# Transformer blocks with a product-key expert layer on one core: order of the first loads, place of the picks' transpositions, output of the first gathered group

## The chip, the cores and the metric

One Trainium2 chip, one core, one program. The time is that of one execution on the device, in microseconds (us). TensorE (PE) multiplies, VectorE (DVE) and ScalarE (ACT) work elementwise, GpSimd (POOL) issues indirect loads, SyncE (SP) issues plain ones; 16 DMA engines move the bytes.

## What is computed

256 tokens of width 1024, a memory of 256 rows, all in float32. A first block adds three branches (a convolution, differential attention, cross attention to the memory), a second one mixes stick-breaking attention and a linear recurrence, and then comes the expert layer, which takes more than half of the time:

```python
h = rms_norm(x, norm_g); mem_h = rms_norm(mem, mem_norm_g)
k, v = jnp.split(mem_h @ w_mem_kv, 2, axis=-1)            # v is the first thing the kernel computes
...
top_s, top_i = lax.top_k(s, PEER_TOPK)                    # per token and head: 16 of 128 keys, twice
best_s, best_pos = lax.top_k(cand_s, PEER_TOPK)           # 16 of 256 pairs
idx = jnp.take_along_axis(cand_i, best_pos, axis=-1)      # 8 heads x 16 picks of 16384 experts
g = jax.nn.softmax(best_s, axis=-1)
u = jnp.take(expert_u, idx, axis=0); v = jnp.take(expert_v, idx, axis=0)
act = jax.nn.gelu(jnp.einsum('td,thkd->thk', xc, u))
y = jnp.einsum('thk,thkd->td', g * act, v)
```

## The kernel before

All work is laid out by a scheduler that fixes one order of instructions for each engine from the program text; each engine then runs its list in order and waits where an operand or a buffer isn't ready.

**Weights of the two blocks.** 94 blocks of weights, two tiles `raw` of 128x1024 (512 KB) each, are loaded by SP (L242). ScalarE rounds a tile to its high part `whi` (L248), VectorE forms the rest `wlo` (L249); four buffers of each are there, so a cast waits until TensorE is through with the tile two blocks back. A product of 256 columns is 48 matmuls of 128x256: high by high, high by low, low by high, over eight channels c (`linN` L343 to L345 for activations as the stationary side, `linT` L309 to L311).

**Start.** SP loads the memory `m_t` (four quarters of 256 KB), the vector `VT` of gains, the two tiles of weight block 0, the input `xr` in two halves, the constants `CT` and `ident`, then further weights. ScalarE scales m_t by its gains to `mgh` (L414), VectorE forms `mgl` (L415). The sums of squares of m_t are eight matmuls against ones (L441) into `stat`; `rstd_of` (L376 to L382) makes `rm` of them, and `tok_scalar` (L422, L424) turns it by token to `rmt`. Four calls of `linN` give the four pieces of `vm`, scaled by `rmt` when ScalarE copies them out (L505). In the second piece lie the sums of squares of xr (L399), then the normed input h, column by column: `nrm` (L409, VectorE), `hh` (L386, ScalarE) and `hl` (L386, VectorE), which the next products need.

**Expert layer.** 160 tokens are done densely: 64 blocks of `u` (`linP`, L290, `ga` takes the gelu) and 64 of `v` (`v_pair`, L1187, into `y`); the weight tiles `w` come in a ring of 13. The gates are applied through one-hot products (`A`, `B`, L1145 to L1165), 40 groups of eight tokens. The 96 other tokens are gathered: GpSimd fetches for each of 96 steps 128 rows of u and of v (L1196, 512 KB a step) into eight slots (three `gat`, five `gat2`), VectorE forms dots (L1203) and then sums (L1219, L1221), in order, over two groups of 32 and 64. Two lists put such work in between the blocks: `bg`, in which each piece has a cost and is popped at 4.6 a block of u, and `advance`, which moves the gathers on.

**Picks.** For each half of the tokens (t = 1, then 0) `bg` holds `logits`, two `decode` (4.3 each, they form the index tiles `IDX`, L1040) and `gates` (3.0), which makes the softmax and then turns both index tiles and the gates by three transpositions on TensorE (L1063 to L1065) and five copies on VectorE (L1067 to L1072).

**End.** `rows_out` is called before the third block of v from the end. For both groups it adds the residual to the sums: eight transpositions of xG (L1247) and a product with `fold` (L1249) into two `lin` tiles of PSUM, copies to a `gat` tile (L1251) and an output DMA from GpSimd (L1252). The dense part is copied from y by ScalarE (L1302) and VectorE (L1304) and written by SP (L1305).

Of the kernel before, what the change touches and what calls it, by code (L numbers as in the profile page):

```python
# [9 lines left out]
F32 = mybir.dt.float32  # L10
# [9 lines left out]
P = 128  # L20
# [168 lines left out]
def build(tc, xT, memT, vec, con, con0, wcat, rgw, keysT, u, v, urow, vrow, out):  # L189
    nc = tc.nc  # L190
    es = ExitStack()
    with es:
# [42 lines left out]
        def prep(i):  # L235
# [4 lines left out]
            for a in range(2):  # L240
                raw = spool.tile([P, 1024], F32, name="raw", bufs=5)
                nc.sync.dma_start(raw, srcs[i][:, a * 1024:(a + 1) * 1024])  # L242
# [89 lines left out]
        def linN(act):  # L332

            ah, al = act
            hs, ls = block()
            ps = lin_ps[0].tile([P, 2, T], F32, name="lin")
            for t in range(2):
                for c in range(8):
                    wh = hs[c // 4].rearrange("p (c j) -> p c j", c=4)[:, c % 4]
                    wl = ls[c // 4].rearrange("p (c j) -> p c j", c=4)[:, c % 4]  # L340
                    xh = ah[:, c, t * P:(t + 1) * P]
                    xl = al[:, c, t * P:(t + 1) * P]
                    nc.tensor.matmul(ps[:, t], xh, wh, start=c == 0, stop=False)  # L343
                    nc.tensor.matmul(ps[:, t], xh, wl, start=False, stop=False)  # L344
                    nc.tensor.matmul(ps[:, t], xl, wh, start=False, stop=c == 7)  # L345
            ahead()
            return ps
# [118 lines left out]
        with ExitStack() as e1:  # L466
# [15 lines left out]
            nc.sync.dma_start(m_t[:, 0:2], memT[:, 0:2])  # L482
            nc.sync.dma_start(VT, vec)
            for k in range(1, 4):
                nc.sync.dma_start(m_t[:, 2 * k:2 * k + 2], memT[:, 2 * k:2 * k + 2])
            prep(0)
            for k in range(2):
                nc.sync.dma_start(x_t[:, 4 * k:4 * k + 4], xT[:, 4 * k:4 * k + 4])
            nc.sync.dma_start(CT, con)
            nc.sync.dma_start(ident, con0[:, :P])  # L490
            mgh, mgl = bigt("mgh", F32R), bigt("mgl", F32R)
            for c in range(NC):
                gain_col(m_t, "mem_norm_g", mgh, mgl, c)
            rm = smt("rm", T, 1)
            stm = statp()
            for c in range(0, NC, 2):
                rms_sq(m_t, stm, c, NC)
# [13 lines left out]
            nc.vector.tensor_scalar_mul(GT[:, 0:1], V("diff_qn_g"), 0.125)  # L511
# [816 lines left out]
```

## Time and profile before

| | us |
|---|---|
| median of three runs | 1287.76 |
| lowest, highest | 1286.37, 1290.27 |
| the profiled execution | 1290.27 |
| its span in the trace | 1288.5 |
| busy: TensorE, VectorE, ScalarE, GpSimd | 1252.9, 936.7, 457.4, 219.3 |

The profile is of one execution. Busy time counts instructions from start to end; matmuls overlap, so a full TensorE shows as a share near 1 and its pace is read from the starts of neighbours or from counts in a window. In a row of the timeline the bracket at the end gives the idle time ahead of it and what ended that.

### The profile page before, as it was taken

The page shows a single profiled execution, that of the slowest core. Times are in us where ns is not written, and L with a number is a line of the kernel's source. Part 1 is how long each engine was busy: PE and PEld are TensorE (multiplying, and loading weights), DVE is VectorE, ACT ScalarE, POOL GpSimd, SP SyncE. Part 2 cuts the span into 40 slices and gives each one's busy share as a digit, 9 for nine tenths or more (in the row PEclk, how much of TensorE's full clock was granted, in tenths as well). Part 3 has the DMA queues.
Part 4 walks back from the last instruction along what each step waited for, and adds up shares of the span by engine and source line. Part 5 has one row for each costly group of instructions (what it writes and reads, how often), then busy time and mean ns, then how long its engine had stood idle before and what let it go on. Part 6 is the DMA issues. An engine that isn't in the chain of part 4 may idle for free.

```text
span 1288.5 us, 24481 instructions
## 1 busy us (share of the span) xinstructions
PE 1252.9 (97%) x9948; PEld 1211.2 (94%) x9948; DVE 936.7 (73%) x1806; ACT 457.4 (35%) x741; POOL 219.3 (17%) x232
## 2 busy tenths in 40 slices
PE   8999999999999999998999999999999999999995
PEld 7999999989999999977999999999999999999884
DVE  6789988888998776865899874678545876454542
ACT  7545677578646556964432111000100000000001
POOL 0000000000000000002013453222342225333330
PEclk9999999999999999999999999999999999999998
DMA  8555544434565664415677899999999999999994
GB/s 287 191 186 188 168 134 131 122 125 148 164 194 167 188 206 156 154 59 200 236 245 220 298 373 408 408 408 404 378 392 334 352 348 407 409 409 409 409 408 155
DMA packets 94865, 340.76 MB, mean 264 GB/s; under 512 B 10576, under 2 KB 12048, under 8 KB 94624
## 3 DMA queue, kind: packets, MB, share of 16 engines
q1 hardware_dynamic: 65312, 232.73, 51.0%
q0 software_dynamic: 29440, 106.46, 21.6%
q8 instruction: 78, 1.28, 0.4%
q14 instruction: 35, 0.29, 0.1%
HBM read 338.01 MB, written 1.05 MB: 263 GB/s over the span
## 4 chain that ended last, share of the span: by engine, by line
PE 43%; issue 19%; DMA 18%; DVE 10%; POOL 6%; ACT 3%; POOLq 0%; SPq 0%; DVEq 0%; ACTq 0%
DMA gat<-in_vrow,gi 13%; PE lin L310 10%; PE lin L309 10%; PE lin L311 10%; POOL gat L1196 5%; DMA gat<-in_urow,gi 5%; PE lin L343 1%; PE lin L345 1%; PE lin L344 1%; DVE gat L1203 1%; DVE acc L1221 1%; DVE wlo L249 1%; PE stat L461 1%; DVE s L997 1%; ACT whi L248 1%
## 5 line engine op out<-in xcount | busy, mean ns | idle before, releaser
L1187 PE MATMUL y<-ga,w 128*128 128x160 f32 x2048 | 292.9, 302 | 5.2 <-DMA w<-in_v 2.5
L1187 PEld LDWEIGHTS y<-ga,w 128*128 128x128 f32 x2048 | 279.9, 190 | 12.5 <-DMA w<-in_v 11.5
L249 DVE TENSOR_TENSOR wlo<-raw,whi 128x1024 fp32r<-128x1024 f32 x188 | 229.3, 1222 | 64.0 <-ACT whi L248 63.3
L290 PE MATMUL lin<-h3f,w 128*128 128x160 f32 x1888 | 265.4, 300 | 0.0
L290 PEld LDWEIGHTS lin<-h3f,w 128*128 128x128 f32 x1888 | 257.7, 190 | 0.2 <-issue 0.2
L248 ACT CAST whi<-raw 128x1024 fp32r<-128x1024 f32 x188 | 196.2, 1049 | 167.0 <-PE lin L310 125.7
L310 PE MATMUL lin<-hl,whi 128*128 128x256 f32 x704 | 200.2, 284 | 0.0
L311 PE MATMUL lin<-hh,wlo 128*128 128x256 f32 x704 | 199.8, 284 | 0.0
L309 PE MATMUL lin<-hh,whi 128*128 128x256 f32 x704 | 199.7, 284 | 0.0
L1221 DVE SCALAR_TENSOR_TENSOR acc<-gat,cG,acc 128x1024 f32<-128x1024 f32 x94 | 120.7, 1284 | 95.9 <-DMA gat<-in_vrow,gi 95.5
L1203 DVE CUSTOM_DVE_ANT_0 gat<-gat,hrow 128x1024 f32<-128x1024 f32 x96 | 116.1, 1223 | 28.6 <-DMA gat<-in_urow,gi 28.6
L311 PEld LDWEIGHTS lin<-hh,wlo 128*128 128x128 f32 x704 | 132.6, 188 | 2.2 <-issue 1.9
L310 PEld LDWEIGHTS lin<-hl,whi 128*128 128x128 f32 x704 | 132.6, 188 | 1.8 <-issue 1.4
L309 PEld LDWEIGHTS lin<-hh,whi 128*128 128x128 f32 x704 | 132.5, 188 | 1.4 <-issue 1.0
L1196 POOL DMA_INDIRECT gat<-in_urow,gi x96 | 101.5, 1058 | 181.2 <-DVE sG L1203 169.4
L1196 POOL DMA_INDIRECT gat<-in_vrow,gi x96 | 93.8, 977 | 166.1 <-DVE acc L1221 137.8
L1176 ACT ACTIVATE ga<-lin 128x320 f32<-128x320 f32 x64 | 28.0, 438 | 243.8 <-PE lin L290 239.5
L950 POOL DMA_DIRECT2D ga<-in_u x10 | 5.4, 545 | 601.3 <-DMA raw<-in_wcat 597.7
L537 DVE SCALAR_TENSOR_TENSOR cacc<-ub,VT,cacc 128x256 f32<-128x256 f32 x240 | 104.0, 480 | 0.0
L1302 ACT COPY ga<-y 128x160 f32<-128x160 f32 x4 | 1.2, 293 | 251.1 <-PE y L1187 251.1
L1165 DVE SCALAR_TENSOR_TENSOR ga<-gp,ga 128x256 f32<-128x256 f32 (+1 forms) x60 | 29.1, 511 | 63.3 <-PE gp L1154 55.9
L310 PE MATMUL lin<-h3lo,whi 128*128 128x256 f32 x128 | 37.6, 294 | 3.0 <-DVE h3lo L386 3.0
(376 smaller groups left out, 2152.0 us busy)
## 6 DMA issues: line engine op xcount, KB each, us to landing
raw<-in_wcat SPq DMA_DIRECT2D x188, 512.0 KB, 4.1
w<-in_v SPq DMA_DIRECT2D x128, 512.0 KB, 13.6
w<-in_u SPq DMA_DIRECT2D x118, 512.0 KB, 9.8
ga<-in_u POOLq DMA_DIRECT2D x10, 512.0 KB, 10.8
gat<-in_urow,gi POOLq DMA_INDIRECT x96, 8.9
gat<-in_vrow,gi POOLq DMA_INDIRECT x96, 18.8
m_t<-in_memT SPq DMA_DIRECT2D x4, 256.0 KB, 3.9
xr<-in_xT SPq DMA_DIRECT2D x2, 512.0 KB, 9.1
```

Source lines behind the costliest of these rows:

```text
L248: nc.scalar.copy(h, raw)
L249: state["sub"] = nc.vector.tensor_sub(l, raw, h.bitcast(F32))
L290: nc.tensor.matmul(ps[:, a], ws[a][:, c * P:(c + 1) * P], x[:, c], start=c == 0, stop=c == 7)
L309: nc.tensor.matmul(ps[:, a], wh, ah[:, c], start=(a, c) in first, stop=False)
L310: nc.tensor.matmul(ps[:, a], wh, al[:, c], start=False, stop=False)
L311: nc.tensor.matmul(ps[:, a], wl, ah[:, c], start=False, stop=(a, c) in last)
L537: nc.vector.scalar_tensor_tensor(cacc[:, c], s, w, cacc[:, c], op0=ALU.mult, op1=ALU.add)
L1165: state["dve"] = nc.vector.scalar_tensor_tensor(g_[:, :, tl], p_, 1.0 / GSCALE, g_[:, :, tl], op0=ALU.mult, op1=ALU.mult)
L1187: nc.tensor.matmul(yT[c // 2][:, c % 2, :D], ws[a][:, c * P:(c + 1) * P], g[:, a], start=False, stop=i == 63 and (a, c % 2) == (1, 1))
L1196: nc.gpsimd.indirect_dma_start(g, None, src, bass.IndirectOffsetOnAxis(gi[:, 0, k:k + 1].bitcast(U32), 0))
L1203: nc.vector.tensor_tensor_reduce(out=g, in0=g, in1=h, scale=1.0, scalar=0.0, op0=ALU.mult, op1=ALU.add, accum_out=sG[:, k:k + 1])
L1221: state["sum"] = nc.vector.scalar_tensor_tensor(acc[m], g, cG[:, k:k + 1], acc[m], op0=ALU.mult, op1=ALU.add)
```

## The change

First, the start. SP loads VT, one quarter of m_t, the first weight tile, two quarters, the second weight tile, the last quarter, both tiles of block 1, and only then xr, CT and ident. The first call of `linN` runs channel by channel (c outside, t inside). The sums of squares of the three later quarters are added on VectorE first, so eight matmuls against ones become four, the last two of them behind the first piece of vm; `rstd_of` and `tok_scalar` follow there. Small preparations (GT, lp) are held back behind a `wlo`, and the table of the second block's recurrence (`la`, `lb`) behind the gate of the merge. Second, `gates` is cut in two: `gates` at a cost of 1.2, a pause of 4.6 for t = 0 in the list, and `turn`, with the transpositions, at 1.8. Third, `rows_out` is cut into `rows_in` (transpositions) and `rows_out` (fold, copies, two output DMAs a group, issued by ScalarE); group 0 goes out in the midst of v, eight steps after its sums are complete, group 1 has `rows_in` at block 61 and `rows_out` behind the dense outputs.

```diff
-        def linN(act):
+        def linN(act, channelwise=False):
...
+            if channelwise:
+                seq = [(t, c) for c in range(8) for t in range(2)]
...
-            nc.sync.dma_start(m_t[:, 0:2], memT[:, 0:2])
             nc.sync.dma_start(VT, vec)
-            for k in range(1, 4):
-                nc.sync.dma_start(m_t[:, 2 * k:2 * k + 2], memT[:, 2 * k:2 * k + 2])
-            prep(0)
+            m_load(0)
+            raws = [load(0, 0)]
+            m_load(1)
+            m_load(2)
+            raws.append(load(0, 1))
+            m_load(3)
+            raws1 = [load(1, a) for a in range(2)]
             for k in range(2):
                 nc.sync.dma_start(x_t[:, 4 * k:4 * k + 4], xT[:, 4 * k:4 * k + 4])
...
+            for k in range(1, 4):
+                q = msq[min(k, 2)]
+                nc.scalar.square(q.rearrange("p (a b) -> p a b", a=2), m_t[:, 2 * k:2 * k + 2])
+                if k > 1:
+                    nc.vector.tensor_add(msq[1], msq[1], q)
...
-            rstd_of(stm[:, :T], 1.0 / 1024, T, out=rm)
-            rmt = tok_scalar(rm, "rmt")
...
-                ps = linN((mgh, mgl))
+                ps = linN((mgh, mgl), j == 0)
+                if j == 0:
+                    for b in range(2):
+                        nc.tensor.matmul(stm[:, :T], ONES, msq[1][:, b * T:(b + 1) * T], start=False, stop=b == 1)
+                    rstd_of(stm[:, :T], 1.0 / 1024, T, out=rm)
+                    rmt = tok_scalar(rm, "rmt")
...
-                bg.append((3.0, gates(t)))
+                bg.append((1.2, gates(t)))
                 if t:
                     bg.append((0.3, rows_index))
+                else:
+                    bg.append((4.6, lambda: None))
+                bg.append((1.8, turn(t)))
...
+            def rows_out(m):
+
+                o_, g, _ = groups[m]
+                o = rows.tile([P, 1024], F32, name="gat", tag="gat", bufs=NB)
+                for n, ps in enumerate(box["out", m]):
+                    sl = slice(n * 512, (n + 1) * 512)
+                    nc.tensor.matmul(ps[:g], fold[:, o_:o_ + g], acc[m][:, sl], start=False, stop=True)
+                    box["copied"] = nc.scalar.copy(o[:g, sl], ps[:g])
+                    nc.scalar.dma_start(out[D * 1024:].rearrange("(r d) -> r d", d=1024)[o_:o_ + g, sl], o[:g, sl])
...
-            if i + 64 == LAST + 1:
-                rows_out()
+            if box["first"] and box["n"] >= NG + GROUPS[0] + NB + MORE + 8:
+                box["first"] = False
+                rows_in(0)
+                rows_out(0)
+            if i == 61:
+                rows_in(1)
             v_pair(i)
...
+        rows_out(1)
```

The order on ScalarE from the statistics of xr (`rv`) to the last column of hh, before (`whi` are casts of weights, `vm` the copies of the pieces):

```order
L376 ACTIVATE rv<-stat,VT 128x256
L377 ACTIVATE rs<-rv 128x256
L378 ACTIVATE rs<-rs 128x256
L379 ACTIVATE rt<-rs 128x256
L248 CAST whi<-raw 128x1024
L505 ACTIVATE vm<-lin,rmt 128x256 x2
L248 CAST whi<-raw 128x1024
L386 CAST hh<-nrm 128x256 x2
L248 CAST whi<-raw 128x1024
L386 CAST hh<-nrm 128x256 x2
L505 ACTIVATE vm<-lin,rmt 128x256 x2
L248 CAST whi<-raw 128x1024
```

Four more hh, two casts of weights and the last two vm follow there. The same place now:

```order
L542 ACTIVATE vm<-lin,rmt 128x256 x2
L387 ACTIVATE rv<-stat,VT 128x256
L388 ACTIVATE rs<-rv 128x256
L389 ACTIVATE rs<-rs 128x256
L390 ACTIVATE rt<-rs 128x256
L254 CAST whi<-raw 128x1024
L397 CAST hh<-nrm 128x256
L254 CAST whi<-raw 128x1024
L397 CAST hh<-nrm 128x256
L542 ACTIVATE vm<-lin,rmt 128x256 x2
L559 ACTIVATE le<-stat 128x2
L397 CAST hh<-nrm 128x256 x6
```

The statistics stand behind the copies of the third piece instead of the first, and six of eight hh behind those of the fourth.

On TensorE, the transpositions of t = 0 among the matmuls of the u blocks, before (`ga_7132` and `ga_7133` are early weight tiles that lie in the place of ga; `gexp` are the gates, A and B the one-hot tiles):

```order
L290 MATMUL lin<-h3f,ga_7132 128x160 x39
L1063 MATMUL gp<-ident,IDX 128x128
L290 MATMUL lin<-h3f,ga_7132 128x160
L290 MATMUL lin<-h3f,ga_7133 128x160 x19
L1064 MATMUL gp<-ident,IDX 128x128
L1065 MATMUL gp<-ident,gexp 128x128
L290 MATMUL lin<-h3f,ga_7133 128x160 x21
L290 MATMUL lin<-h3f,w 128x160 x256
L1154 LDWEIGHTS A
```

And now:

```order
L296 MATMUL lin<-h3f,ga_7129 128x160 x39
L1108 MATMUL gp<-ident,IDX 128x128
L296 MATMUL lin<-h3f,ga_7129 128x160
L296 MATMUL lin<-h3f,ga_7130 128x160 x34
L1109 MATMUL gp<-ident,IDX 128x128
L1110 MATMUL gp<-ident,gexp 128x128
L296 MATMUL lin<-h3f,ga_7130 128x160 x6
L296 MATMUL lin<-h3f,w 128x160 x256
L1202 LDWEIGHTS A
```

The second and third have moved 15 matmuls back; the first stands where it stood.

The last rows on ScalarE, before (`ga` takes the dense outputs from y, `gat` the gathered ones):

```order
L1302 COPY ga_7132<-y_7144 128x160
L1302 COPY ga_7132<-y_7145 128x160
L1302 COPY ga_7132<-y_7146 128x160
L1302 COPY ga_7132<-y_7147 128x160
L1251 COPY gat<-lin 32x512 x2
L1251 COPY gat<-lin 64x512 x2
```

And now:

```order
L1304 COPY gat<-lin 32x512 x2
L1305 DMA out<-gat 32x512 x2
L1361 COPY ga_7129<-y_7141 128x160
L1361 COPY ga_7129<-y_7142 128x160
L1361 COPY ga_7129<-y_7143 128x160
L1361 COPY ga_7129<-y_7144 128x160
L1304 COPY gat<-lin 64x512
L1305 DMA out<-gat 64x512
L1304 COPY gat<-lin 64x512
L1305 DMA out<-gat 64x512
```

The first group's copies stand ahead of the dense ones, and each half of a group has an output DMA of its own on ScalarE.

## Rows read from the trace of the kernel before

**Rows 1.** The page: busy time, share of the span, instructions.

```profile
PE 1252.9 (97%) x9948; PEld 1211.2 (94%) x9948; DVE 936.7 (73%) x1806; ACT 457.4 (35%) x741; POOL 219.3 (17%) x232
```

**Rows 2.** Timeline of TensorE, start: start us, us, engine, line, operation, tiles, count.

```profile
20.17 0.60 PE L422 MATMUL stat<-ONES,rm 1*128 1x1 f32 x4
20.70 0.39 PE L343 MATMUL lin<-whi,mgh 128*128 128x256 f32 x1
...
22.24 1.02 PE L399 MATMUL stat<-sqs,ONES 128*128 128x256 f32 x4
22.91 0.47 PE L343 MATMUL lin<-whi,mgh 128*128 128x256 f32 x1
```

**Rows 3.** DMA, 0 to 20 us (slices of 0.5), median us to landing; SP's issue.

```profile
GB/s 0 0 0 29 193 116 257 349 367 373 242 209 254 250 233 242 344 344 344 385 401 369 401 434 418 418 401 411 409 418 426 410 410 410 401 410 401 418 426 410
...
xr<-in_xT SPq DMA_DIRECT2D x2, 512.0 KB, 9.1
...
4.04 0.98 SPq L488 DMA_DIRECT2D xr<-in_xT  x2
```

**Rows 4.** Timelines of ScalarE, VectorE and TensorE around the first use of h.

```profile
37.74 1.05 ACT L248 CAST whi<-raw 128x1024 fp32r<-128x1024 f32 x1 [1.60 <-PE lin L345]
38.69 0.71 ACT L386 CAST hh<-nrm 128x256 fp32r<-128x256 f32 x2
...
37.43 0.88 DVE L409 SCALAR_TENSOR_TENSOR nrm<-xr,VT,rs 128x256 f32<-128x256 f32 x2
38.83 1.22 DVE L249 TENSOR_TENSOR wlo<-raw,whi 128x1024 fp32r<-128x1024 f32 x1 [0.52 <-ACT whi L248]
39.97 0.75 DVE L386 TENSOR_TENSOR hl<-nrm,hh 128x256 fp32r<-128x256 f32 x2
...
39.08 0.36 PE L309 MATMUL lin<-hh,whi 128*128 128x256 f32 x1
```

**Rows 5.** Two stretches (columns as in rows 6), and TensorE's timeline at the picks.

```profile
610.00:615.00 5.00, 4.81 (x22) 4.81 (x23) 5.00 (x12) 4.03 (x5) 0.00 (x0) 0.50 1.03 423
615.00:620.00 5.00, 5.00 (x43) 5.00 (x42) 2.09 (x2) 2.08 (x3) 0.00 (x0) 0.95 0.99 398
...
731.56 0.47 PE L1063 MATMUL gp<-ident,IDX 128*128 128x128 f32 x1 [2.91 <-DVE IDX L1040]
```

**Rows 6.** Stretches: us; busy PE, PEld, DVE, ACT, POOL; PEclk, DMA share, GB/s.

```profile
1070.00:1200.00 130.00, 130.00 (x948) 128.35 (x947) 68.16 (x55) 0.00 (x0) 52.68 (x55) 1.00 1.03 409
1200.00:1260.00 60.00, 55.91 (x369) 50.46 (x368) 29.27 (x23) 0.00 (x0) 18.87 (x20) 1.00 1.03 409
```

**Rows 7.** Gathers: DMA queues 1100 to 1160 (packets, MB, share); timelines of GpSimd, VectorE.

```profile
q1 hardware_dynamic: 3364, 12.24, 51.3%
q0 software_dynamic: 3359, 12.23, 51.0%
...
1134.80 0.94 POOL L1196 DMA_INDIRECT gat<-in_vrow,gi  x1 [1.62 <-DVE acc L1221]
...
1148.60 1.28 DVE L1221 SCALAR_TENSOR_TENSOR acc<-gat,cG,acc 128x1024 f32<-128x1024 f32 x1 [1.29 <-DMA gat<-in_vrow,gi]
```

**Rows 8.** The end: timelines of TensorE, ScalarE and GpSimd; output DMAs' KB and landing.

```profile
1269.18 3.53 PE L1187 MATMUL y<-ga,w 128*128 128x160 f32 x24 [0.83 <-DMA w<-in_v]
1273.61 1.96 PE L1247 MATMUL lin<-ident,xG 128*64 128x128 f32 x16 [0.90 <-ACT gat L1251]
1275.41 1.88 PE L1249 MATMUL lin<-acc,fold 128*64 128x512 f32 x4
...
1276.47 0.58 ACT L1251 COPY gat<-lin 64x512 f32<-64x512 f32 x1 [2.43 <-PE lin L1249]
...
1278.20 0.59 POOL L1252 DMA_DIRECT2D out<-gat  x1 [3.31 <-ACT gat L1251]
...
out<-gat POOLq DMA_DIRECT2D x1, 256.0 KB, 3.0
out<-gat POOLq DMA_DIRECT2D x1, 128.0 KB, 2.2
```

More of the change, by code (lines that the diff above doesn't have):

```diff
@@ L233, in prep_plain, with load, prep @@
             prepared[i] = ws
-        def prep(i):
+        def load(i, a):
+            raw = spool.tile([P, 1024], F32, name="raw", bufs=5)
+            nc.sync.dma_start(raw, srcs[i][:, a * 1024:(a + 1) * 1024])
+            return raw
+        def prep(i, raws=None, between=None):
             if i >= NW:
@@ L240, in prep @@
             for a in range(2):
-                raw = spool.tile([P, 1024], F32, name="raw", bufs=5)
-                nc.sync.dma_start(raw, srcs[i][:, a * 1024:(a + 1) * 1024])
+                raw = load(i, a) if raws is None else raws[a]
+                if between is not None:
+                    between(a)
                 h = spool.tile([P, 1024], F32R, name="whi", bufs=4)
@@ L336, in linN @@
             ps = lin_ps[0].tile([P, 2, T], F32, name="lin")
[L337 to L345, printed above, removed]
+            if channelwise:
+                seq = [(t, c) for c in range(8) for t in range(2)]
+                first, last = seq[:1], seq[-1:]
+            else:
+                seq = [(t, c) for t in range(2) for c in range(8)]
+                first, last = [(0, 0), (1, 0)], [(0, 7), (1, 7)]
+            for t, c in seq:
+                wh = hs[c // 4].rearrange("p (c j) -> p c j", c=4)[:, c % 4]
+                wl = ls[c // 4].rearrange("p (c j) -> p c j", c=4)[:, c % 4]
+                xh = ah[:, c, t * P:(t + 1) * P]
+                xl = al[:, c, t * P:(t + 1) * P]
+                nc.tensor.matmul(ps[:, t], xh, wh, start=(t, c) in first, stop=False)
+                nc.tensor.matmul(ps[:, t], xl, wh, start=False, stop=False)
+                nc.tensor.matmul(ps[:, t], xh, wl, start=False, stop=(t, c) in last)
             ahead()
@@ L768, in build @@
             la, lb, sp8, sm8 = (smt(n, 4, 1) for n in ("la", "lb", "sp8", "sm8"))
-            nc.scalar.activation(la, lam, AF.Abs)
+            with tc.issue_after(state["gate"].ins):
+                nc.scalar.activation(la, lam, AF.Abs)
             nc.scalar.activation(la, la, AF.Exp, scale=-1.0)
             nc.scalar.activation(la, la, AF.Ln, bias=1.0)
-            nc.vector.tensor_scalar(lb, lam, 0.0, -1.0, op0=ALU.min, op1=ALU.mult)
+            with tc.issue_after(state["gate"].ins):
+                nc.vector.tensor_scalar(lb, lam, 0.0, -1.0, op0=ALU.min, op1=ALU.mult)
             nc.vector.tensor_add(la, la, lb)
@@ L1061, in f, with turn @@
                     nc.vector.tensor_mul(gg_, gg_, zz.unsqueeze(2).to_broadcast([P, 8, 16]))
+                return f
+            def turn(t):
+                def f():
+                    gg_ = box[t]
                     pt = gps.tile([P, 512], F32, name="gp", tag="gp")
@@ L1301, in build @@
             o = ga[0][:, 2 * b:2 * b + 2]
-            nc.scalar.copy(o[:, 0], yT[b][:, 0, :D])
+            with tc.issue_after(first.ins):
+                nc.scalar.copy(o[:, 0], yT[b][:, 0, :D])
             with tc.issue_after(state["sum"].ins):
```

62 lines of the change are left out of this document (35 added, 27 removed).

## The prediction

> **What bounds the kernel now.** I read the page first: TensorE is busy for 1252.9 of 1288.5 us, ScalarE for 35% of them, so only TensorE's idle and slow stretches and the two ends can give time [rows 1]. Then TensorE's timeline. At the start the second piece of `vm` begins at 20.70 [rows 2]. In the pick stage it waits 2.91 us for an index tile, until 731.56, and behind an earlier wait the granted clock stands at 0.50 from 610 to 615, the lower of its two levels (1.2 against 2.4 GHz) [rows 5]. Then the table by stretches: from 1070 to 1260 the DMA engines move 409 GB/s throughout, and from 1200 TensorE is short of weights, 55.91 of 60 us busy [rows 6]. So the last 190 us are bound by bytes: what is still to be loaded when TensorE leaves the last one-hot group is paid at 409 GB/s. Last the end: the last y matmul is done at 1272.7, but the output of the gathered rows is issued only at 1278.20 and lands 3.0 us later, at 1281.2; the span closes 7.3 us behind that [rows 8].
>
> The sum is made against the profiled execution, 1290.27 us, of which the span is 1288.5. It is the slowest of the three runs, 2.51 above the median of 1287.76; I assume that the same differences hold for the median.
>
> **Start: an earlier first piece, a later h.** VT, the first quarter of m_t and the first weight tile now go ahead of the rest. Summing the half-microsecond slices, 0.97 MB (VT 0.18, a quarter 0.26, a weight tile 0.52) have moved by 5.5 us, and 2.02 MB (two more quarters and the second weight tile) by 9.4. The two halves of xr, issued at 4.04 and 4.5 and landing 9.1 us later, come about 1.4 us behind their bytes, so the weight tiles land at about 6.9 and 10.8 [rows 3]. From a cast's start to its `wlo` it takes 1.09 + 1.22 us (37.74, 38.83) [rows 4]: `wlo` is whole at 9.2 and 13.1. A matmul of 128x256 costs 0.218 us at the low clock (22 in 4.81 us) and 0.116 to 0.12 at the high one (43 in 5.00) [rows 5]. I take the low clock until the second tile is whole, 18 of the 48 matmuls, and the high one for the other 30, to 16.7. Two sums of squares follow (0.67 us, from 22.24 to 22.91), so the next piece starts at 17.4 instead of 20.70: 3.3 us earlier. Turning rm into a token scalar (0.53, from 20.17 to 20.70) now falls into the third piece [rows 2], which leaves 2.8 at the end of the fourth. At the high clock throughout it would be 3.5, at the low one through all 48 (10.5 us) nothing.
>
> This gain meets a new wait. Before, the sum of squares of xr ran in the second piece, and the eight columns of hh and hl were made two by two between the casts of weights; the last two began at 38.69, and TensorE went into the first matmul with hh at 39.08 without a pause [rows 4]. Now that sum stands behind the third piece, and in ScalarE's order a weight cast stands before the first hh and another before the second. These casts wait for a buffer: the first for matmul 36 of 48 of the fourth piece, the second for its last one. The row of before shows the same gate: a cast at 37.74, released by TensorE, 1.3 us before 39.08. Call the end of the fourth piece E. The first hh begins at E-0.3, and its hl, behind `wlo`, is done at E+1.4; the second cast runs from E+0.1 to E+1.1, and the second hl is done at E+2.9; then VectorE owes six more columns at 0.44 for nrm and 0.38 for hl, 4.9 us, to E+7.8 [rows 4]. In the new order TensorE interleaves two weight blocks and needs a column every six matmuls: without waits it is through 46 of them at E+5.6, now at E+8.1. The wait is 2.5 us (1.5 if the hand-overs overlap better, 3.5 if each costs 0.15 more). Start in all: -2.8 + 2.5 = **-0.3** us, between -2.0 and +3.5.
>
> The four small ScalarE and VectorE operations that move to the merge gate, with four more table loads, lie where ScalarE has room, being busy for 35% of the span [rows 1]: 0; without that cover they would cost about a wait of the kind just worked out.
>
> **Picks.** For the tokens of t=1 nothing moves. For t=0 the first transposition stays behind 39 matmuls with the same tile, and VectorE's work ahead of its IDX is the same, so the wait of 2.91 us [rows 5] stays, with the slow clock behind it. The other two move 15 matmuls back, and four dots go ahead of the second IDX; both sides of that hand-over come later by much the same. The first one-hot product is 256 matmuls further, so nobody waits for what VectorE does then. Term: 0, from -0.5 to +1. What shifts is the row of gathered sums: when VectorE takes up the last one-hot group it has added 9 rows instead of 10. One row is 0.524 MB, at 409 GB/s [rows 6] **+1.3** us (0 to +2.6).
>
> **End.** The first group's 128 KB goes out in the stretch bound by bytes: +0.3. The 16 transposition records of the second group (1.96 us) [rows 8] move into block 61 of v, where TensorE idles for 4.1 of 60 us [rows 6] and has data late anyway: **+0.2** (0 to +1). Behind the last y matmul, at 1272.7, there is then only the fold, the copies and ScalarE's own output DMAs. A copy begins 1.06 us behind its half of the fold (1275.41, 1276.47) and takes 0.58: 1273.8 to 1274.4. An issue costs at most 0.59 (POOL's), so the second copy is done at 1275.5, and a landing of 2.2, as for the 128 KB output, gives 1277.7 against 1281.2 [rows 8]: **-3.5** (-4.2 to -2.9).
>
> **Sum:** -0.3 + 1.3 + 0.3 + 0.2 - 3.5 = -2.0: 1288.3 against 1290.27, and **1285.8 us** against the median.
>
> **The rivals.**
> *The wait for hh doesn't come.* The columns are ready in time and the start keeps 2.8: 1285.8 - 2.5 = 1283.3. For it speaks that before had no pause there; against it ScalarE's order, in which seven of eight hh stand behind the end of the piece.
> *The wait is dearer: the clock falls in it.* TensorE would work about half the time for some 4 us, in short pieces. From 610 to 615 the low clock let 22 matmuls through where the next 5 us took 43, 21 x 0.116 = 2.4 us lost [rows 5]: 1288.2. Against it: from 1200 to 1260 TensorE pauses often, and the table shows 1.00 [rows 6]. The Trainium skill's page "TensorE: Matmul & The Clock Gate", section "A second HAM failure mode: psum-queue depth-cycling", says that small idles between groups of matmuls can be frequent enough to make the clock swing between its levels; by it this rival would be the forecast. The stretch from 1200 to 1260 speaks against it, though its pauses are smaller.
> *The pick's first wait goes too.* If VectorE had its IDX 2.91 us earlier [rows 5], 1285.8 - 2.9 = 1282.9. The order on both engines says that it doesn't.
> *Slower: the borrowed slot stalls the gathers.* The first group's output takes one of eight slots for a turn. The gather that was issued at 1134.80 then needs the slot of the row two issues before it, whose sum is formed at 1148.60 [rows 7]; sums are formed in order, so the rows behind it wait too, and for some 15 us, six issues of 2.56, nothing is issued. If the weights don't use that time, five rows' worth is lost: 5 x 1.28 = 6.4, 1292.2. It decides if the gathers' queue runs empty while no weight load is outstanding. From 1100 to 1160 both queues have work and move the same, 12.24 and 12.23 MB [rows 7], so I expect the weights to take the time. The Trainium skill's page "DMA: Bandwidth & Descriptors", section "Queues, rings and completion order", says that each DMA engine goes round the queues that have work for it; by that rule the price is 0 as long as weight loads are queued, and the even split agrees.
>
> **How the numbers follow.** Chances: the forecast 0.52, no wait for hh 0.15, the clock falls 0.14, the pick's wait goes 0.06, the slot 0.13. About 0.3%, 3.9 us, is what a measurement of this kernel can tell from no change: faster is below 1283.9, slower above 1291.6. Faster: most of the no-wait case, the pick's case, and a fifth of the forecast's (start at -2.0, no row lost): 0.29. Slower: three quarters of the slot's case and a little of the others: 0.12. The rest is 0.59. The range goes from the no-wait case less 1.0 (no row lost there), 1282.3, to the forecast with its start at the dear end, 3.8 more, and a little of a second row, 1289.9.
>
> **What would show it.** The first weight matmul before 9 us and the second piece at about 17.4; behind the fourth piece several pauses on TensorE, released by VectorE's hl, 2.5 us together, and the granted clock at 1.00 or not; the wait for IDX still near 2.9; the gathers with a hole of some 15 us after the middle of v while DMA stays at 409 GB/s; no transposition behind the last y, and the last output landing 5.0 us behind it instead of 8.5. I am wrong if the first piece ends as late as before, if the pauses at hh are missing, or if DMA falls below 409 GB/s before the last weights.

## The result and the profile after

The changed kernel takes 1297.23 us in the median of nine runs, the kernel before, on the same chip, 1289.01: a ratio of 1.0066, with a 95% interval from 1.005 to 1.0083. It is slower by some 8 us, where no change that could be told was forecast (1285.8 us, 1282.3 to 1289.9). The profiled execution, the slowest of the nine, took 1299.06 us; its span is 1297.1.

The page's line of busy time answers to [rows 1]; then come TensorE's waits by what ended them (us in total, times, longest):

```profile
PE 1254.8 (97%) x9940; PEld 1216.6 (94%) x9940; DVE 936.9 (72%) x1808; ACT 462.4 (36%) x745; POOL 223.2 (17%) x230
```

```profile
PE lin L1303 <- DVE acc L1269: 10.4, 1, 10.4
PE gp L1108 <- DVE IDX L1080: 3.7, 2, 3.4
PE att L684 <- ACT sig L683: 2.5, 2, 1.4
PE lin L315 <- ACT sig L714: 1.5, 1, 1.5
PE lin L316 <- DVE hl L397: 1.2, 2, 0.7
```

TensorE is as busy as before. Three of these waits are new: for the last sum of gathered rows (10.4 us), for `sig` in the attention (2.5 and 1.5), and for `hl` at the start (1.2). The two pauses at the start, then windows of the start, the pick, and a stretch of [rows 6] (columns as there); the last row, in a fence of its own, is of the kernel before:

```profile
38.91 0.39 PE L316 MATMUL lin<-hl,whi 128*128 128x256 f32 x1 [0.72 <-DVE hl L397]
40.38 0.38 PE L316 MATMUL lin<-hl,whi 128*128 128x256 f32 x1 [0.50 <-DVE hl L397]
40.00:42.00 2.00, 1.53 (x7) 1.26 (x8) 1.95 (x7) 0.81 (x2) 0.00 (x0) 0.84 0.88 266
42.00:44.00 2.00, 2.00 (x11) 2.00 (x11) 1.93 (x6) 0.80 (x2) 0.00 (x0) 0.50 0.61 217
44.00:46.00 2.00, 2.00 (x16) 2.00 (x16) 1.38 (x4) 0.80 (x2) 0.00 (x0) 0.81 0.01 2
46.00:48.00 2.00, 2.00 (x19) 2.00 (x18) 0.00 (x0) 0.98 (x1) 0.00 (x0) 1.00 0.00 0
746.00:750.00 4.00, 4.00 (x17) 4.00 (x17) 4.00 (x7) 0.00 (x0) 1.69 (x1) 0.50 0.33 119
1200.00:1260.00 60.00, 60.00 (x444) 60.00 (x444) 27.64 (x22) 0.00 (x0) 24.69 (x27) 1.00 1.03 409
```

```profile
42.00:44.00 2.00, 2.00 (x20) 2.00 (x19) 0.40 (x1) 0.49 (x1) 0.00 (x0) 1.00 0.62 188
```

From 40 to 46 us TensorE does 7, 11 and 16 matmuls where the kernel before did 20 in each 2 us: the granted clock is at its lower level (0.50) behind the pauses for `hl`, in this execution. From 1200 on it is full, 60.00 of 60, where before it was short of weights [rows 6]; what is late now are the gathers. The end, answering to [rows 8]:

```profile
1269.60 19.78 DVE L1269 SCALAR_TENSOR_TENSOR acc<-gat,cG,acc 128x1024 f32<-128x1024 f32 x15 [1.30 <-DMA gat<-in_vrow,gi]
1289.44 3.67 PE L1303 MATMUL lin<-acc,fold 128*64 128x512 f32 x4 [10.39 <-DVE acc L1269]
1293.15 0.58 ACT L1304 COPY gat<-lin 64x512 f32<-64x512 f32 x1 [1.13 <-PE lin L1303]
1293.76 0.47 ACTq L1305 DMA_DIRECT2D out<-gat  x1
```

The last y is done at 1279.0, the last sum at 1289.4, the last issue begins at 1293.76, and the span ends 3.3 us behind it; before it ended 10.3 us behind the last issue (1278.20 to 1288.5).

Matching TensorE's records of both traces in order gives where it fell behind the kernel before (times of that kernel): 2.5 us at 51, 3.3 from 116 to 250, 7.5 at 350, 9.8 at 404, 12.6 at 602, 15.1 at 747, 16.2 at the last one-hot group. From there to the end of the span the changed kernel needs 214.0 us, the kernel before 221.7. So 16 us were lost in places where the prediction had put nearly nothing, and the end won 7.7 where it had put 3.5. Each of these lags, here and below, compares one execution with one other. Part of them changes from execution to execution, since a stretch at the lower clock isn't there in each: the one from 611.4 to 614.8 us, which goes with most of the step at 602, is in none of the other traces with the swap told of below.

### The profile page after: what moved, and what is told of

The parts are those of the page before. It is cut to its first block, busy times and chain, and to the rows that moved or that the text cites. A ratio compares the mean times of both kernels' runs of the same rounds, so it can differ in the third digit from the quotient of the medians.

```text
span 1297.1 us, 24467 instructions
## 1 busy us (share of the span) xinstructions
PE 1254.8 (97%) x9940; PEld 1216.6 (94%) x9940; DVE 936.9 (72%) x1808; ACT 462.4 (36%) x745; POOL 223.2 (17%) x230
## 3 DMA queue, kind: packets, MB, share of 16 engines
q8 instruction: 78, 1.28, 0.4%
## 4 chain that ended last, share of the span: by engine, by line
PE 71%; DMA 11%; DVE 10%; ACT 4%; issue 3%; POOL 1%; SPq 0%; POOLq 0%; DVEq 0%; ACTq 0%
PE y L1235 14%; PE lin L296 13%; PE lin L315 10%; PE lin L316 10%; PE lin L317 10%; DMA gat<-in_vrow,gi 5%; DMA gat<-in_urow,gi 4%; DVE acc L1269 2%; PE gp L1202 1%; PE lin L356 1%; PE lin L354 1%; PE lin L355 1%; DMA w<-in_v 1%; DVE wlo L255 1%; POOL gat L1244 1%
## 5 line engine op out<-in xcount | busy, mean ns | idle before, releaser
L1235 PE MATMUL y<-ga,w 128*128 128x160 f32 x2048 | 285.6, 300 | 0.0
L1244 POOL DMA_INDIRECT gat<-in_urow,gi x96 | 105.9, 1103 | 174.1 <-DVE sG L1251 162.2
```

The source lines that it names most:

```text
L1235: nc.tensor.matmul(yT[c // 2][:, c % 2, :D], ws[a][:, c * P:(c + 1) * P], g[:, a], start=False, stop=i == 63 and (a, c % 2) == (1, 1))
L1244: nc.gpsimd.indirect_dma_start(g, None, src, bass.IndirectOffsetOnAxis(gi[:, 0, k:k + 1].bitcast(U32), 0))
```

## The experiments

Every kernel was compared with the kernel before on the same chip. Differences in us are between the medians of such a comparison.

**The four parts alone.** The diff falls into the start (with `linN`), the chain of `la` and `lb`, the picks, and the outputs; each was put alone into the kernel before.

> Only the start: first piece with its two halves of weights interleaved, sums of squares behind the third piece, the gains between the casts; nothing of the gates, the picks or the outputs. Theory (the loss is collected on TensorE before the gathered rows begin, and the start causes most of it, because the whole schedule behind it is laid out anew): TensorE reaches the last one-hot group 9 to 11 us later than in the kernel before, in three places: the first use of hh with its fallen clock (net +2.4 at 51 us), 310 to 350 us (+4.3, ScalarE's order in the differential attention), 578 to 602 us (+2.6); time 9 to 10 us above the kernel before (ratio 1.007 to 1.008). Rival (the loss is the borrowed slot and the late first output behind the gathers; what TensorE loses earlier is hidden by the transfers): no more than the +2.4 of the hh wait, ratio 0.999 to 1.002.

> Only the chain of small operations on rg_lambda_2 held back to the merge gate. Theory: in the changed kernel TensorE fell 1.8 to 2.0 us further behind between 391 and 404 us, where that chain and its table loads of 1.28 us stand on ScalarE; alone it costs the same 2 us at that place and nothing elsewhere (ratio 1.001 to 1.002). Rival (the lag there is another piece of the new order, ScalarE has room for the chain): TensorE's lag stays at 0 through 404 us, ratio 1.000.

> Only the picks' transpositions moved back by half a u block. Theory: TensorE loses 1 to 3 us between 731 and 830 us: the wait for IDX of t=0 stays (2.9 to 3.4 us) and the clock is lower behind it, and one row less is added when the last one-hot group is taken up; ratio 1.001 to 1.003. Rival (picks are neutral and what was lost there in the changed kernel was the shifted overlap with the rest): lag below 0.5 us at the last one-hot group, ratio 1.000 or a little below.

> Only the outputs: the first group's in mid v, the second's transpositions in v block 61, its copies and DMAs on ScalarE. Theory (the tail works and the hole in the gathers costs little, since the weights use the bytes): TensorE reaches the last one-hot group as before (lag 0), the gathers show a hole of 20 us or more behind the first output, DMA stays near 409 GB/s, the time is 3 to 7 us under the kernel before (ratio 0.995 to 0.998). Rival (the borrowed slot stalls the gathers and the last sums of rows come late): TensorE waits 5 to 10 us for the last sum, and the time is as before or above it (ratio 1.000 to 1.005).

| part alone | forecast | us | ratio, 95% interval |
|---|---|---|---|
| start | -0.3 | +13.5 | 1.0117, 1.0092 to 1.0143 |
| la, lb | 0 | +0.6 | 1.0004, 0.999 to 1.0018 |
| picks | 0, and 1.3 for a row of gathers | +4.9 | 1.0039, 1.0024 to 1.0054 |
| outputs | -3.0 | -8.0 | 0.9938, 0.9914 to 0.9962 |

The start carries the loss, and more of it than expected (four runs, 1295.90 to 1305.22 us; the profiled one is the fastest). In its trace TensorE falls behind by 3.0 us between 220 and 350 and by 1.7 at 400 us, with the same three waits for `sig` as in the whole change. The step at 400 us, which I had put down to `la` and its table loads, is there without them and is missing where they were moved alone: that reading was wrong. The outputs alone beat both kernels.

**The swap inside the start.** The diff shown ahead leaves out one edit that the prediction passed over. `linN` got its second loop order for the first piece, and in rewriting it the second and third matmul of each group changed places for every call:

```diff
                     nc.tensor.matmul(ps[:, t], xh, wh, start=c == 0, stop=False)
-                    nc.tensor.matmul(ps[:, t], xh, wl, start=False, stop=False)
-                    nc.tensor.matmul(ps[:, t], xl, wh, start=False, stop=c == 7)
+                    nc.tensor.matmul(ps[:, t], xl, wh, start=False, stop=False)
+                    nc.tensor.matmul(ps[:, t], xh, wl, start=False, stop=c == 7)
```

n_alone is the kernel before with this alone; s_oldorder is the whole start without it (but for the first piece).

> The kernel before, with one edit: in the products with activations as the stationary side, the second and third matmul of each group of three change places (high by high, low by high, high by low). Theory (this swap, which came along with the new first piece, moves the point at which a weight tile comes free; the scheduler then lays out ScalarE's list anew from 230 to 350 us, and the extra table loads and late casts there cost TensorE what the changed kernel lost in the middle): the waits of TensorE for sig near 320, 334 and 337 us appear (1.4, 1.1, 1.5 us), lag +4 to +5 at 350 us, another +1.7 at 404, in all +6 to +8 us (ratio 1.005 to 1.006). Rival (the new start shifts everything behind it in time, and this is what rearranges the middle): no such waits, lag 0 at 400 us, ratio 0.999 to 1.001.

> The whole start of the change, but the order of the three matmuls as in the kernel before everywhere except in the first piece. Theory: the middle is that of the kernel before (no waits for sig at 310 to 350, no step at 404); what is left is the start: the first use of hh with waits and a fallen clock, lag +2 to +3 behind 50 us counted from the first matmul with hh; ratio 1.000 to 1.003. Rival (the new start rearranges the middle): lag +6 at 410 us as with the whole start, ratio 1.009 or more.

The swap alone costs 8.8 us (1.0067, 1.0044 to 1.0091), as much as the whole change; TensorE's lag goes from 0 at 240 us to 4.4 at 365 and 6.1 at 415, so the step at 400 us is its work too. Of the 3 us that come later in this trace, 2.5 come at the picks, where s_oldorder, without the swap, loses 2.7 and s_alone, with it, gains 0.7; they can't be put down to it. The start without the swap costs 5.0 (1.0035, 1.0019 to 1.0051); its lag stays at 2.4 us from 47 to 604 us, the middle being that of the kernel before. ScalarE's list in the kernel before, then in n_alone, around the copy of `sig` that TensorE needs next, and TensorE's wait for it:

```profile
312.90 1.28 ACT L377 ACT_TABLE_LOAD   x1
314.84 1.28 ACT L378 ACT_TABLE_LOAD   x1
317.97 0.46 ACT L645 COPY sig<-att 128x384 f32<-128x384 f32 x1
328.26 0.48 ACT L645 COPY sig<-att 128x384 f32<-128x384 f32 x1
```

```profile
311.23 1.28 ACT L377 ACT_TABLE_LOAD   x1
313.06 1.03 ACT L248 CAST whi<-raw 128x1024 fp32r<-128x1024 f32 x1
314.11 1.28 ACT L664 ACT_TABLE_LOAD   x1
315.40 0.60 ACT L664 ACTIVATE gate<-lin 128x512 f32<-128x512 f32 x1
316.00 1.28 ACT L572 ACT_TABLE_LOAD   x1
318.60 0.46 ACT L645 COPY sig<-att 128x384 f32<-128x384 f32 x1
331.34 1.04 ACT L248 CAST whi<-raw 128x1024 fp32r<-128x1024 f32 x1 [1.77 <-PE lin L310]
332.29 0.47 ACT L645 COPY sig<-att 128x384 f32<-128x384 f32 x1
...
319.11 0.70 PE L646 MATMUL att<-sig,vd 128*128 128x256 f32 x2 [1.41 <-ACT sig L645]
332.81 0.70 PE L646 MATMUL att<-sig,vd 128*128 128x256 f32 x2 [1.07 <-ACT sig L645]
335.24 0.58 PE L309 MATMUL lin<-hh,whi 128*128 128x256 f32 x1 [1.51 <-ACT sig L676]
```

`gate` now stands between two operations of other tables, so there are three loads of 1.28 us ahead of the first `sig` instead of two, and a cast of weights as well; the second `sig` stands behind a cast that waits for TensorE itself. From 227 us on, where `linN` makes the values of the differential attention, ScalarE's list is laid out anew (casts change places between 27 and 40 us too, without a lag). With the swap a group ends on `wlo` and not on `whi`, so a tile of `whi` comes free one matmul sooner, and a cast is put ahead of a copy of `vd`; all that follows shifts. These rows show the waits; that just this cast sets off the rest is read from the order and wasn't tested.

**The whole change without the swap, as a check of the sum.**

> The whole change, but with the three matmuls in the order of the kernel before (everywhere except in the first piece). Theory (the swap made the loss in the middle, and the parts add up): start +2.4 to +5, small chain +0.6, picks +2 to +5, outputs -8: 1285 to 1291, ratio 0.997 to 1.002, no waits for sig between 310 and 350 us. Rival (the parts don't add up, the middle is lost as soon as anything ahead of it moves): above 1293, ratio 1.004 or more.

It gives +0.2 us (1.0003, 0.9986 to 1.0019) and no wait for `sig`: 8.4 us below the changed kernel, about what the swap cost alone. Its profiled execution took 1292.46 us, 3.6 above its median, and TensorE loses 5 us in it from 757 to 765; where that comes from stays open. The single parts sum to +11.0 against 8.2 measured; each has an interval of 2 to 3 us to either side, so this isn't a contradiction, and not a proof that they add up exactly.

**The start's wait for hh.** Here xr is loaded ahead of the second weight block, and then, in s_hh_ahead, the statistics and columns of h are also written ahead of the first copies of vm:

```diff
+            for k in range(2):
+                nc.sync.dma_start(x_t[:, 4 * k:4 * k + 4], xT[:, 4 * k:4 * k + 4])
             raws1 = [load(1, a) for a in range(2)]
-            for k in range(2):
-                nc.sync.dma_start(x_t[:, 4 * k:4 * k + 4], xT[:, 4 * k:4 * k + 4])
...
                     rmt = tok_scalar(rm, "rmt")
+                    rms_cols(x_t, "norm_g", hh, hl)
                 for t in range(2):
...
-                if j == 0:
-                    rms_cols(x_t, "norm_g", hh, hl)
```

> As the last one, but the two loads of xr go ahead of the second weight block's. Theory of the start (hh is late because its sum of squares, its statistics and its columns stand behind weight casts, not because xr lands late): the waits for hl at 38 to 41 us and the low clock stay, or shrink by half at most, lag +1 to +2.5; ratio 1.000 to 1.003. Rival (xr's late landing is the cause): no wait for hl, the clock stays at 1.00, the start gains 1 to 2 us (ratio 0.998 to 1.000).

> The start of the change with the old order of matmuls and xr loaded ahead of the second weight block, and now also the sums of squares and the columns of hh written ahead of the copies of the first piece of vm. Theory (TensorE's waits for hl at 38 to 43 us and the low clock behind them are what the start loses; the load order itself gains nothing measurable): hh and hl are made before TensorE asks for them, no wait for hl, the low clock from 40 to 46 us is gone, the time is that of the kernel before within 0.15% (ratio 0.9985 to 1.0015). Rival (the start's loss comes from its loads and its longer first piece, not from hh): a loss as with xr ahead alone, ratio 1.0015 or more. If the copies of vm come too late instead, TensorE waits for a lin tile in the third piece and the lag at 50 us grows.

With xr first one wait for `hl` of two is left, and the loss goes from 5.0 to 2.6 us (1.0015, 1.0004 to 1.0026). With h ahead there is no wait for `hl`, but the copies of vm come too late, as the last sentence of the expectation feared, and the gain is gone (+5.6 us, 1.0045, 1.003 to 1.0059). The first wait in each, s_x_first and then s_hh_ahead:

```profile
42.07 0.39 PE L316 MATMUL lin<-hl,whi 128*128 128x256 f32 x1 [0.68 <-DVE hl L401]
```

```profile
35.08 0.42 PE L354 MATMUL lin<-whi,mgh 128*128 128x256 f32 x1 [2.43 <-ACT vm L547]
34.00:38.00 4.00, 2.92 (x14) 2.92 (x15) 3.75 (x10) 3.09 (x9) 0.00 (x0) 0.66 0.68 216
```

Behind this pause the clock falls (0.66 from 34 to 38 us). Behind the shorter pauses of the changed start it falls in one trace of four, that of the changed kernel. In s_alone, with the same start and nearly the same pauses, it stays at 1.00:

```profile
38.76 0.40 PE L316 MATMUL lin<-hl,whi 128*128 128x256 f32 x1 [0.72 <-DVE hl L397]
40.23 0.38 PE L316 MATMUL lin<-hl,whi 128*128 128x256 f32 x1 [0.48 <-DVE hl L397]
42.00:44.00 2.00, 2.00 (x17) 1.77 (x16) 1.93 (x6) 0.81 (x2) 0.00 (x0) 1.00 0.59 217
```

So the lower clock is not what these starts have in common. A start that loses nothing was not found; what it would be worth stays open.

**The picks' pause.** The 4.6 between `gates` and `turn` is left out.

> The picks cut in two as in the change, but without the pause of 4.6 between the two parts for t = 0, so that the transpositions go back to about their old place. Theory (the loss of the picks alone, 4.9 us, comes from the pause: five dots go ahead of the second index tile, two of them wait for their gathers, and TensorE waits 2.2 us a second time): one wait of 2.9 to 3.4 us for the first IDX, none above 0.5 for the second, ratio 0.999 to 1.0015. Rival (cutting it in two costs by itself, since the copies behind the transpositions come later): ratio 1.003 or more, as with the pause.

+2.4 us (1.0024, 1.001 to 1.0039), between the two. The picks with the pause, on TensorE and then on VectorE:

```profile
730.88 0.33 PE L1068 MATMUL gp<-ident,IDX 128*128 128x128 f32 x1 [3.35 <-DVE IDX L1040]
742.90 0.33 PE L1069 MATMUL gp<-ident,IDX 128*128 128x128 f32 x1 [2.18 <-DVE IDX L1040]
738.72 1.23 DVE L1211 CUSTOM_DVE_ANT_0 gat<-gat,hrow 128x1024 f32<-128x1024 f32 x1 [1.47 <-DMA gat<-in_urow,gi]
741.40 1.23 DVE L1211 CUSTOM_DVE_ANT_0 gat<-gat,hrow 128x1024 f32<-128x1024 f32 x1 [0.78 <-DMA gat<-in_urow,gi]
742.55 0.29 DVE L1040 TENSOR_TENSOR IDX<-eq 128x128 f32<-128x128 f16 x1
```

The second index tile comes at 742.55, behind five dots instead of one, of which two wait for their gathers; before it came at 736.59, and TensorE asked for it at 738.8:

```profile
738.79 0.27 PE L1064 MATMUL gp<-ident,IDX 128*128 128x128 f32 x1
736.59 0.29 DVE L1040 TENSOR_TENSOR IDX<-eq 128x128 f32<-128x128 f16 x1
```

Without the pause the second wait is gone. What the pause costs isn't shown by that: the two intervals overlap, and from 720 to 770 us TensorE falls back by 3.6 us in the trace without it and by 3.7 with it; without it the clock is lower (0.52 from 730 to 735, before 0.66), and fewer matmuls are done behind the picks (27 from 750 to 755 us, before 39):

```profile
750.00:755.00 5.00, 4.54 (x27) 3.73 (x27) 4.33 (x10) 0.54 (x2) 3.61 (x4) 1.00 0.96 322
```

The traces differ behind the picks instead. At the last one-hot group 115 gathers have been issued with the pause, 116 without it, 117 before, and from there to the end it takes 223.5, 221.2 and 221.7 us. The rest stays open. In kernels whose picks were those of before, TensorE's lag changed there by -0.9 us (la and lb alone) to +2.7 (s_oldorder): the first IDX is waited for 2.7 to 3.4 us in most, and in n_alone and s_oldorder 4.3 and 4.5 us for a `ga` of ScalarE ahead of it and then 0.8 and 1.0. The clock differs as well: from 730 to 735 it is 0.66 before, 1.00 in l_alone and 0.50 in o_pool_dma.

**The end.** t_queue_only is the kernel before with ScalarE issuing both output DMAs of the gathered rows; q_outputs_gpsimd_last the changed outputs with GpSimd issuing the last two.

```diff
-                    nc.gpsimd.dma_start(out[D * 1024:].rearrange("(r d) -> r d", d=1024)[o_:o_ + g], o[:g])
+                    nc.scalar.dma_start(out[D * 1024:].rearrange("(r d) -> r d", d=1024)[o_:o_ + g], o[:g])
```

> The kernel before, with one word changed: the two output DMAs of the gathered rows are issued by ScalarE and not by GpSimd; everything stays where it was. Theory (most of the 8 us that the outputs gained alone is the close of the program: behind the last landing the span ran on for 7.3 us where GpSimd had issued the last DMA, and for 1.3 us where ScalarE had): 5 to 7 us under the kernel before (ratio 0.9946 to 0.996), and the last landing comes no earlier than before. Rival (the gain is the work moved out of the tail, as the forecast had it: transpositions, copies, issue): no more than the 0.2 us between the issues, ratio 0.999 to 1.000.

> The outputs as in the change, but the second group's two DMAs issued by GpSimd and not by ScalarE. Theory (close of the program): 5 to 7 us are lost against the outputs alone, ratio 0.998 to 0.9995 against the kernel before; the span closes 6 to 8 us behind the last landing. Rival (work moved out of the tail): as with the outputs alone, 0.994 to 0.995.

One word wins 5.7 us (0.996, 0.9938 to 0.9983); the outputs with GpSimd at the end keep 2.6 of their 8.0 (0.9981, 0.9971 to 0.9991). The last copy, the last issue and the span of t_queue_only:

```profile
core 0 of [0], span 1282.0 us
...
1277.28 0.58 ACT L1251 COPY gat<-lin 64x512 f32<-64x512 f32 x1 [0.28 <-PE lin L1249]
1277.89 0.53 ACTq L1252 DMA_DIRECT2D out<-gat  x1
```

The issue is 0.3 us earlier than in [rows 8], the span ends 6.5 earlier. Behind GpSimd's last DMA the program takes 10.3 us to close, behind ScalarE's 4.1. So it is in all eighteen traces: 10.2 to 10.3 us where GpSimd issued the last output, 3.3 to 4.1 where ScalarE did, also where GpSimd had issued the first group's (o_pool_dma, 3.7).

**The borrowed slot.** o_pool_dma lets GpSimd issue the first group's two DMAs (the last two stay with ScalarE); o_own_tile leaves all with ScalarE and copies the first group into a piece of `ga` that v has done with:

```diff
-                    nc.scalar.dma_start(...)
+                    (nc.scalar if m else nc.gpsimd).dma_start(...)
```

```diff
-                o = rows.tile([P, 1024], F32, name="gat", tag="gat", bufs=NB)
+                if m:
+                    o = rows.tile([P, 1024], F32, name="gat", tag="gat", bufs=NB)
+                else:
+                    o = ga[0][:, 8:15].rearrange("p a b -> p (a b)")[:, :1024]
```

> Only the outputs, and the two output DMAs of the first group issued by GpSimd, in the queue of the gathers, and not by ScalarE; the borrowed slot stays. Theory (the hole of 27.8 us in the gathers is made by the output DMAs, which ScalarE issues 33 us behind their copies, since the issue waits for weight loads, and not by the slot itself): the output goes out within 3 us of its copies, the hole is below 6 us, the last sum is formed as early as the last y, TensorE's wait of 7.8 us at the end falls below 3, time 1.5 to 5 us under that of the outputs alone (ratio 0.990 to 0.993 against the kernel before). Rival (the slot makes the hole, and the bytes set the end anyway): hole 15 us or more, time as with the outputs alone (0.994).

> Only the outputs as in the change (ScalarE issues all four DMAs), but the first group's rows are copied into a piece of ga that v no longer needs, and not into a slot of the gathers' ring. Theory (the borrowed slot leaves a hole of 27.8 us in the gathers, but the weights take these bytes and the total sets the end; the queue of the last DMA made most of the gain): no hole above 4 us, y ends later and the last sum earlier, and the time is within 1.5 us of the outputs alone and of those with GpSimd's DMAs (ratio 0.992 to 0.995 against the kernel before). Rival (the slot's rival of the prediction, at its price): 5 us or more faster than the outputs alone, ratio below 0.990.

In the outputs alone the two DMAs are issued 33 us behind their copies, and the gathers stand still, while TensorE later waits for the sums:

```profile
1136.32 0.57 ACT L1256 COPY gat<-lin 32x512 f32<-32x512 f32 x1 [0.28 <-PE lin L1255]
1169.85 1.58 ACTq L1257 DMA_DIRECT2D out<-gat  x2
1176.57 0.94 POOL L1196 DMA_INDIRECT gat<-in_vrow,gi  x1 [27.80 <-DMA out<-gat]
1271.48 3.68 PE L1255 MATMUL lin<-acc,fold 128*64 128x512 f32 x4 [7.82 <-DVE acc L1221]
1150.00:1176.00 26.00, 26.00 (x192) 25.31 (x191) 7.81 (x7) 0.00 (x0) 0.00 (x0) 1.00 1.03 409
```

The DMA engines move 409 GB/s in the hole. o_pool_dma splits it into one of 5.5 and one of 13.6 us, so the slot itself makes a hole too; o_own_tile has none, and TensorE's wait for the last sum is gone in it. There ScalarE issues its two DMAs 1.5 to 1.6 us behind their copies (1135.17 and 1137.72), so an issue by ScalarE doesn't cost 33 us by itself. In both traces each of these issues comes 0.07 to 0.08 us behind the landing of a load of weights that reports to the same semaphore: SP issued these loads at 1156.24 and 1158.80 in o_alone, at 1116.75 and 1118.92 in o_own_tile. The times are 0.9927 (0.9908 to 0.9945) and 0.9921 (0.9892 to 0.995), against 0.9938 (0.9914 to 0.9962) with the whole hole: it costs at most a few us, and none that these runs could tell.

**The best version.** o_pool_dma once more, and beside it the same with the start of s_hh_ahead.

> The outputs with GpSimd issuing the first group's two DMAs once more, beside the next one: 0.991 to 0.9945 as before.

> The mended start (no wait for hh) and the outputs with GpSimd issuing the first group's DMAs. If the parts add up and the mended start is neutral: 0.991 to 0.995, no different from the outputs alone. If the start's shorter first piece is worth the 2.8 us that the prediction gave it once hh doesn't wait: 0.988 to 0.991.

0.9917 (0.9893 to 0.9942) and 0.9963 (0.995 to 0.9976): that start takes back 6.5 us. The outputs alone, with GpSimd's DMAs for the first group or with a tile of its own, are the best found: 1278.4 to 1279.4 us, 9 to 11 below the kernel before and some 18 below the change.

## Why the prediction was wrong

**What bounds the kernel.** Right that the last 190 us are bound by bytes. 158 loads of 0.524 MB were open at the last one-hot group in the changed kernel; at 409 GB/s from 1083.1 they end at 1285.5, and the last gather landed at 1287.1. So what TensorE loses ahead of that point comes back at the end, and there lay the 16 us. The nine traces with the old outputs bear this out: from the last one-hot group to the end they take 220.0 to 223.5 us, whether TensorE was there 2.9 us sooner than in the profile of before or 9.2 later.

**The step that failed first: the middle.** The sum had no term between 60 and 700 us. The swap in `linN` was read as a change of the first piece. It isn't a cost of its own (in n_alone TensorE has no lag up to 240 us, behind several such products); it moved the point from which the scheduler lays out ScalarE's list. 8.8 us came with it, 6.1 of them seen by 415 us in its trace. The differences of order from 230 to 350 us could be read ahead of the run; I looked only at the three places that the change names. One sign of them stood in the prediction: its "four more table loads" were all put down to the operations at the merge gate, at no cost. Moving la and lb alone makes three more (30 instead of 27), the swap alone makes one (28), and that one stands ahead of `sig`.

**Start.** The gain of 2.8 was counted from a late execution. In eleven profiled executions with the old start the first matmul with `hh` begins between 36.45 and 39.08 us, 37.5 in the mean, and the profile of before is the latest; in the four with the changed start and its load order it is 37.26 to 38.61, mean 37.8. The first weight matmul did come earlier (9.56 in the changed kernel, against 11.93), but that piece is slower: the next begins at 18.5, not at 17.4. So the gain was nothing: the step that failed at the start is "3.3 us earlier". The wait for `hh` came where it was forecast, in two pauses. From the first `hh`, 96 matmuls with h take 11.35 us before and 14.2 to 14.3 in the three other traces of this start, 2.8 to 3.0 us more at a full clock: 1.3 to 1.7 us of pauses, the rest in matmuls that start 0.2 us apart instead of 0.12. Forecast was 2.5, so that term was sized about right. In the changed kernel it is 15.2 us; the rival "the clock falls" came there, and cost 0.8 us more than the same start at a full clock in s_alone, not 2.4. I had set the stretch from 1200 to 1260 against it, whose pauses I called smaller; 21 of 22 are (at most 0.13 us), but one of 1.64 us is among them, and the clock stays at 1.00 behind it as well. The Trainium skill's page "TensorE: Matmul & The Clock Gate", section "A second HAM failure mode: psum-queue depth-cycling", has small idles between groups of matmuls make the clock swing. The trace of the changed kernel agrees; s_alone, with the same pauses and no fall, does not.

**The small operations at the merge gate.** Right: 0 was forecast, +0.6 measured, not told from 0.

**Picks.** "Both sides of that hand-over come later by much the same" failed: TensorE came 2 us later, VectorE 6, for the four more dots ahead of the second IDX and the two waits for their gathers. The 1.3 us for a row of gathers that comes later has a counterpart in the trace of p_alone: two gathers fewer have been issued at the last one-hot group, and the stretch behind it is 1.8 us longer. In the whole change this second wait doesn't show; there the clock is down from 746 to 750 (17 matmuls in 4 us), and the lag grows by 2.3; without the swap it shows (0.86 us in after_oldorder).

**The slot.** The rival's mechanism came, longer than forecast (25.7 us in the changed kernel, not 15), and through the late issue as well as through the slot: with the issue at once, holes of 5.5 and 13.6 us are left (o_pool_dma). Its price did not: as expected, the weights took the time, 409 GB/s in the hole of the outputs alone. The Trainium skill's page "DMA: Bandwidth & Descriptors", section "Queues, rings and completion order", by which the engines go round the queues that have work, agrees.

**End.** Sized wrongly: -3.5 up to the landing, measured -8.0 alone. Work moved out of the tail is the smaller part, 2.6; 5.7 came from the queue. The prediction carried the 7.3 us behind the landing over as a constant; they belonged to GpSimd's DMA. And the fold came dearer: behind TensorE's wait for the last sum its four matmuls take 3.67 us instead of 1.88 [rows 8], at the lower clock:

```profile
1289.40:1293.10 3.70, 3.66 (x4) 0.75 (x4) 0.91 (x4) 0.58 (x1) 0.00 (x0) 0.50 0.60 177
```

So a gain more than twice as large as forecast met losses of 13.5 and 4.9 us, where the sum had a gain of 0.3 and a loss of 1.3.

## What to carry to other kernels

Where a scheduler lays out the whole program, compare its order from end to end, not only where the edit is: a swap of two equal matmuls cost more here than any part that was meant, and it is first seen as a table load or a cast ahead of something that TensorE needs. Take the base of a small term from several executions, since one trace of the start was off by 1.5 us. And look at which engine issues the last DMA: moving it from GpSimd to ScalarE was worth more than all the work moved out of the tail.

## What the runs showed of the hardware

- The close of the program depends on the queue of the last output DMA: 10.3 us from issue to the end of the span with GpSimd (before), 4.1 with ScalarE (t_queue_only, one word changed).
- In the changed kernel, behind two pauses of 0.72 and 0.50 us, ahead of the matmuls at 38.91 and 40.38, TensorE's granted clock fell to 0.50, the lower level; from 46 to 48 us it was at 1.00 again. Behind pauses of 0.72 and 0.48 us in s_alone, and of 1.64 us at 1208 in the kernel before, it stayed at 1.00. So a pause of this size brought the clock down in one execution and not in another.
- Two output DMAs on ScalarE, whose copies were done at 1136.9, were issued at 1169.85 in the stretch bound by bytes (o_alone). In o_own_tile, where the loads ahead of them on the same semaphores were issued some 40 us earlier, ScalarE issued them 1.5 to 1.6 us behind their copies; GpSimd issued the second 0.3 us behind its copy (1136.97, in o_pool_dma). That the issue waits for such a load to land is read from the times of the landings and wasn't tested by a run.
